# Moving the weight pages of a one-core encoder block to 96 bytes past a 128-byte boundary

## The chip, the core and the metric

The kernel runs on one core of a Trainium2 chip. The metric is the device time of one execution in microseconds, the median of several runs. One further execution is profiled: its page and its trace give, for every instruction of every engine, when it started and how long it took. TensorE does the matmuls (PE in the profile; its weight loads are listed apart as PEld), VectorE is DVE, ScalarE is ACT, GpSimd is POOL and SyncE, which issues most transfers, is SP.

## The reference, cut to what matters

One layer of an encoder over 512 tokens of width 2048, all in float32:

```
h = rms_norm(x)
q_a, k_a, v_a, q_g, k_g, v_g, r_g, gate_lr = split(h @ w_in)
y_a = banded softmax attention(q_a, k_a, v_a)         # 16 heads of 64
y_g = rms_norm(gated linear attention(q_g, k_g, v_g, gate)) * silu(r_g)   # 4 heads
x = x + concat(y_a, y_g) @ w_out
u = causal_conv(rms_norm(x) @ w_ffn_up);  u_gate, u_val = split(u)
x = x + (gelu(u_gate) * u_val) @ w_ffn_down           # inner width 5632
x = x + sigmoid(rms_norm(x) @ w_ple_gate) * (p @ w_ple_proj)
return rms_norm(x)
```

Nearly all of the work is the products of a weight matrix with the 512 tokens. The change alters no arithmetic.

## The kernel before, in words

**Precision.** Each float32 operand of a large product is split in two parts that TensorE reads as its fast float32 type (`F32R`): a rounded high part and the low rest. A product is then three matmuls: high by high, high by low, low by high. ACT writes the high part of a weight page (`wh`), DVE the low part (`wl`) as the difference (`prep_high`, line 447, and `prep_low`, line 470).

**Pages.** A page is a tile of 128 partitions by 1024 float32, 4096 bytes in each partition. The pool `pages` (line 49) holds 17 of them, one behind the other: `r0` to `r7` for raw weights, `u0`, `u1`, `c0` for results, and `h0` to `h2` and `l0` to `l2` for the high and low parts of the weights that TensorE reads. Seven more pages (`c1`, `x0`, `x1`, `u2`, `u3`, `c2`, `r8`, the tuple `LATE`) lie in the pool `late` at the right end of the memory and are opened after the attention.

**The first 330 us.** `vproj` (line 228) computes values with the weights streaming: in lines 250 to 252 the moving operand is a page `wh` or `wl`, 512 columns wide, and the stationary one is 128 columns of an input tile `h1` (pool `h`, 16 tiles of 4096 bytes, `slot`, line 203). There are 4 calls (two column halves for each of two value matrices), each with 16 blocks of the inner dimension, 4 blocks of tokens and 3 matmuls. `proj` (line 137, through `mm3`, line 132) is turned round: the page is stationary, an input tile is the moving operand, 512 columns wide; 8 calls of 16 blocks and 3 matmuls. One more product, `plr` (lines 1077 to 1080), reads its stationary columns from a page at steps of 128 bytes.

**The rest.** All later weight products run by a seven-product Strassen scheme in stages: `in`, `wo`, `up`, three `dn`, `pg` (class `Stage`, line 312). A unit is two blocks of 128 output rows. Its operands from the token side (`R11`, `R21`, `N2`, `N1`, `T3`, `R22`, `T4`) were combined beforehand, stored to device memory, and are loaded per stage into tiles of 128 x 2 x 1024 float32, 8192 bytes in each partition: six in the pool `xa` at the right, eight in the pool `xb` at the left (`xtile`, line 299), `xb` taking over the room of `h`. `product` (line 482) issues the matmuls: for an ordinary product three passes over `kb` inner blocks (8, or 7 in two of the `dn` stages), moving 256 columns of an operand tile over 128 columns of `wh` or `wl` (line 513); in the units between the first two and the last two of a stage, three of the seven products are joined (line 502): high by (high and low) in one matmul of 512 columns from two places of the operand tile, then low by high in 256 columns (line 504).

In the last stage three tiles of the pool `xa` that are no longer needed serve as pages for the weights of the last products (`EARLY`, line 936, and lines 1270 to 1273; their name is `last`).

**Order.** Each engine takes its instructions in the order in which the kernel issues them; from line 1248 on the order on DVE, ACT and TensorE is that of the loop over `steps` (line 1250), where the weights of step i + 2 are prepared before the product of step i.

**Where the tiles lie.** The left side grows upward from constants and scratch; the right side grows downward from the end. Two tiles exist only to set addresses: `shim` (240 float32, 960 bytes, line 1036) at the right end before everything else there, and `pad` (8 float32, 32 bytes, line 1223) at the start of `xb`. The byte offsets in each partition come to:

| tiles | first byte | past a multiple of 128 | past a multiple of 512 |
|---|---|---|---|
| `pages` | 15360 | 0 | 0 |
| input tiles `h1` | 84992 | 0 | 0 |
| operand tiles in `xb` | 85024 | 32 | 32 |
| operand tiles in `xa`, so `last` too | 179232 | 32 | 32 |
| `late` pages | 150560 | 32 | 32 |
| attention tiles `Q`, `Kh`, `Kl` | 152352 and on | 32 | 288 |

Within a product all offsets go in steps of 512 bytes (stationary) and 1024 or 4096 bytes (moving), so a whole product has one pair of places.

Of the kernel before, what the change touches and what calls it, by code (L numbers as in the profile page):

```python
# [8 lines left out]
F32 = mybir.dt.float32  # L9
# [5 lines left out]
P = 128  # L15
# [27 lines left out]
def encoder_block(ctx: ExitStack, tc: tile.TileContext, A, out):  # L43
    nc = tc.nc
# [4 lines left out]
    pg = ctx.enter_context(tc.tile_pool(name="pages", bufs=1))  # L49
# [153 lines left out]
    def slot(i, name, dt=F32R):  # L203
        return hp.tile([P, 2, T], dt, tag=f"h{i}", name=name)

    pairs = [pg.tile([P, 2, T], F32, tag=t, name=f"pair_{t}") for t in PAIR_TAGS]

    def xslot(i, name):
# [54 lines left out]
    xa, xb = [], []  # L263
# [126 lines left out]
    def issue():  # L390
        kept, i = 0, 0
        while i < len(wanted):
            unit, name = wanted[i]
            if len(free) <= kept:
                return
            if name[-1] == "*":
                kept += 1
                i += 1
                continue
            wanted.pop(i)  # L400
            n = unit.stage.kb * P
            t = raw_page(unit, name)[:, :n]
            src = lambda q: unit.stage.weights(unit.u, q)
            if name[0] == "L":
                nc.sync.dma_start(t, src(name))
            else:
                nc.sync.dma_start(t, src("L21"))
                nc.gpsimd.dma_start(t, src("L22" if name == "S1" else "L11"), accum_op=ALU.add)  # L408
# [35 lines left out]
    def prep(i, own=None):  # L444
        prep_low(prep_high(i, own))
# [587 lines left out]
            (nc.scalar if c else nc.sync).dma_start(vad[4 * c:4 * c + 4, :, t].rearrange("b p v -> p b v"),  # L1033
                              vstage[c, t].rearrange("p (b v) -> p b v", b=4))

    shim = ctx.enter_context(tc.tile_pool(name="shim", bufs=1, side="right")).tile([P, 240], F32, tag="shim", name="shim")
    nc.gpsimd.memset(shim, 0.0)
    with ExitStack() as mix:
        vp = mix.enter_context(tc.tile_pool(name="v", bufs=1, side="right"))
# [180 lines left out]
    def operands_left():  # L1220
        hctx.close()
        xb.append(ctx.enter_context(tc.tile_pool(name="xb", bufs=1, reuse_waits="tile")))
        pad = xb[0].tile([P, 8], F32, tag="pad", name="pad")
        nc.gpsimd.memset(pad, 0.0)
        for op in ("N1", "T3", "R22", "T4"):
            for g in range(2):
                front.load(op, g)
        free.extend(("r0", "r1", "r2"))
        issue()
        prep(0)  # L1230
        prep(1)
        for g in range(2):
            front.split("N1", g)

    values_a(1, operand_step, operands_left)
    pctx.close()
    pp_ = ctx.enter_context(tc.tile_pool(name="banks", bufs=1, space=PSUM, reuse_waits="tile"))
# [194 lines left out]
```

## Time and profile before

| | us |
|---|---|
| three runs | 2314.81, 2318.54, 2322.06 |
| median of the runs | 2318.54 |
| span of the profiled execution, first to last instruction | 2315.0 |

The profiled execution's own time is its span and a little around it; the span lies within the spread of the three runs, 3.5 us under their median. The page gives, for each engine, its busy time and share of the span; then the span in slices; the transfers; the chain of work that ended last; and the costliest groups of instructions with count, total busy time and mean duration. Matmuls overlap one another on TensorE, so the duration of one (279 ns in many groups) is not what it costs: that is the distance from its start to the start of the next, which the timeline of the engine gives. There a row is a run of equal instructions: start of the first, time from there to the end of the last, what it is, and how many.

### The profile page before, as it was taken

What the parts mean: (1) busy time and instruction counts of PE and PEld (TensorE: products, weight loads), DVE (VectorE), ACT (ScalarE), POOL (GpSimd) and SP (SyncE); (2) the same over time, 40 slices, a digit from 0 to 9 for tenths busy, and PEclk for the clock granted to TensorE, in tenths of its full rate; (3) what the DMA queues carried; (4) which work ended last, traced back from release to release, by engine and by line L of the source; (5) the groups of instructions that cost most, each with busy time, mean ns of one, the idle gap of its engine ahead of it and who ended that gap; (6) DMA issues with size and microseconds to landing.
All of it is one profiled execution on the core that took longest, in us unless ns stands there. A gap on an engine that the chain in (4) does not pass through costs nothing.

```text
span 2315.0 us, 42243 instructions
## 1 busy us (share of the span) xinstructions
PE 2269.1 (98%) x16564; PEld 2122.6 (92%) x16564; DVE 1957.4 (85%) x2753; ACT 1295.4 (56%) x1894; POOL 143.1 (6%) x180
## 2 busy tenths in 40 slices
PE   9999999999999999999999999999999999999996
PEld 8878889999989999999999999999999999999995
DVE  7556358888779888999999999999898797999997
ACT  6344356777555565555555555555564554656655
POOL 0000000000000000000000000000000100000100
PEclk9999999999999999999999999999999999999998
DMA  6522486666978977787877777777866967879994
GB/s 221 195 76 88 168 286 168 177 182 185 314 244 269 309 219 201 214 220 213 219 211 214 206 218 207 218 210 217 261 213 222 316 216 250 282 241 331 273 288 160
DMA packets 195464, 516.48 MB, mean 223 GB/s; under 512 B 20896, under 2 KB 72352, under 8 KB 195264
## 3 DMA queue, kind: packets, MB, share of 16 engines
q1 hardware_dynamic: 165184, 421.49, 51.9%
q0 software_dynamic: 23616, 84.95, 20.8%
q10 hardware_dynamic: 6464, 7.34, 0.9%
q8 instruction: 130, 2.13, 0.4%
q14 instruction: 70, 0.57, 0.1%
HBM read 435.05 MB, written 76.55 MB: 221 GB/s over the span
## 4 chain that ended last, share of the span: by engine, by line
PE 86%; DVE 6%; DMA 4%; ACT 2%; issue 2%; ACTq 0%; DVEq 0%; SPq 0%; POOL 0%; POOLq 0%
PE accA L65 39%; PE accC L65 20%; PE accB L65 10%; PE v L250 2%; PE v L251 2%; PE v L252 2%; DVE wl L65 1%; DMA s<-in_w_blk 1%; DVE u L65 1%; PE pp L65 1%; PE py L65 1%; PE ptr L65 1%; DVE s L65 1%; PE psc L65 1%; PE pk L134 1%
## 5 line engine op out<-in xcount | busy, mean ns | idle before, releaser
L65 DVE TENSOR_TENSOR wl<-s,wh 128x1024 fp32r<-128x1024 f32 (+1 forms) x365 | 437.3, 1199 | 47.3 <-ACT wh L65 46.3
L65 ACT ACTIVATE wh<-l 128x1024 fp32r<-128x1024 f32 (+1 forms) x308 | 318.8, 1037 | 174.9 <-PE accC L65 110.2
L65 ACT ACTIVATE wh<-s 128x1024 fp32r<-128x1024 f32 (+1 forms) x365 | 377.6, 1037 | 48.1 <-DVE s L65 31.8
L65 DVE TENSOR_TENSOR wl<-l,wh 128x1024 fp32r<-128x1024 f32 (+1 forms) x308 | 367.8, 1194 | 39.8 <-ACT wh L65 39.5
L65 ACT ACTIVATE u<-accA 128x256 f32<-128x256 f32 x290 | 109.4, 377 | 339.1 <-PE accA L65 338.9
L65 DVE TENSOR_TENSOR s<-s,l 128x1024 f32<-128x1024 f32 (+1 forms) x192 | 229.5, 1195 | 13.9 <-DMA s<-in_w_blk 12.7
L65 PE MATMUL accA<-up_T,wh 128*128 128x256 f32 (+1 forms) x1088 | 178.6, 313 | 0.2 <-ACT u L65 0.2
L65 PEld LDWEIGHTS accA<-up_T,wh 128*128 128x128 f32 x1088 | 150.1, 188 | 11.4 <-ACT u L65 0.4
L65 DVE SCALAR_TENSOR_TENSOR cv<-u,cw,cv 128x511 f32<-128x511 f32 (+1 forms) x176 | 131.5, 747 | 3.1
L408 POOL DMA_DIRECT2D s<-in_w_up x88 | 75.1, 853 | 788.4 <-DVE u L65 256.7
L65 DVE TENSOR_TENSOR u<-u,accC 128x256 f32<-128x256 f32 x158 | 66.1, 418 | 44.2 <-PE accC L65 41.5
L251 PE MATMUL v<-wv_l,h 128*128 128x512 f32 x256 | 100.5, 392 | 0.0
L250 PE MATMUL v<-wv_h,h 128*128 128x512 f32 x256 | 100.3, 392 | 0.0
L252 PE MATMUL v<-wv_h,h 128*128 128x512 f32 x256 | 99.9, 391 | 0.0
L65 PE MATMUL accA<-up_T,wl 128*128 128x256 f32 x704 | 96.3, 279 | 0.0
L65 ACT ACTIVATE cv<-u,cw 128x512 f32<-128x512 f32 x88 | 67.1, 810 | 51.9 <-DVE u L65 51.9
L65 PEld LDWEIGHTS accA<-up_T,wl 128*128 128x128 f32 x704 | 91.2, 188 | 3.7
L65 PE MATMUL accA<-dn_T,wh 128*128 128x256 f32 (+1 forms) x616 | 90.4, 296 | 2.8 <-ACT wh L65 2.8
L65 PE MATMUL accB<-up_R,wh 128*128 128x512 f32 (+1 forms) x384 | 91.2, 380 | 1.9 <-DVE up_R L65 1.3
L65 PE MATMUL accA<-up_R,wh 128*128 128x256 f32 x704 | 89.7, 279 | 0.0
L65 PE MATMUL accA<-up_N,wh 128*128 128x256 f32 x704 | 89.3, 279 | 0.1
L65 PE MATMUL accC<-up_N,wh 128*128 128x256 f32 x704 | 89.2, 279 | 0.0
(386 smaller groups left out, 5123.2 us busy)
## 6 DMA issues: line engine op xcount, KB each, us to landing
l<-in_w_up SPq DMA_DIRECT2D x132, 512.0 KB, 5.1
s<-in_w_up SPq DMA_DIRECT2D x88, 512.0 KB, 4.6
s<-in_w_up POOLq DMA_DIRECT2D x88, 512.0 KB, 5.7
l<-in_w_dn SPq DMA_DIRECT2D x56, 448.0 KB, 5.0
l<-in_w_blk SPq DMA_DIRECT2D x36, 512.0 KB, 5.1
l<-in_w_out SPq DMA_DIRECT2D x28, 512.0 KB, 5.2
l<-in_w_dn SPq DMA_DIRECT2D x28, 512.0 KB, 5.3
s<-in_w_blk SPq DMA_DIRECT2D x24, 512.0 KB, 4.5
```

Source lines behind the costliest of these rows:

```text
L65: ins = f(*args, **kw)
L134: nc.tensor.matmul(po, whi, act[:, 1, :], start=False, stop=False)
L250: nc.tensor.matmul(ps[t], h1[kt][:, 0, sl], wh, start=kt == 0, stop=False)
L251: nc.tensor.matmul(ps[t], h1[kt][:, 0, sl], wl, start=False, stop=False)
L252: nc.tensor.matmul(ps[t], h1[kt][:, 1, sl], wh, start=False, stop=kt == KD - 1)
L408: nc.gpsimd.dma_start(t, src("L22" if name == "S1" else "L11"), accum_op=ALU.add)
```

## The change

A tile `lead` of 24 float32, 96 bytes in each partition, is put at the start of the pool `pages` and set to zero once. `pad` grows from 32 to 64 bytes and `shim` shrinks from 960 to 832 bytes.

```
+    lead = pg.tile([P, 24], F32, tag="lead", name="lead")
+    nc.gpsimd.memset(lead, 0.0)
     pairs = [pg.tile([P, 2, T], F32, tag=t, name=f"pair_{t}") for t in PAIR_TAGS]
...
-    shim = ctx.enter_context(tc.tile_pool(name="shim", bufs=1, side="right")).tile([P, 240], F32, tag="shim", name="shim")
+    shim = ctx.enter_context(tc.tile_pool(name="shim", bufs=1, side="right")).tile([P, 208], F32, tag="shim", name="shim")
     nc.gpsimd.memset(shim, 0.0)
...
-        pad = xb[0].tile([P, 8], F32, tag="pad", name="pad")
+        pad = xb[0].tile([P, 16], F32, tag="pad", name="pad")
         nc.gpsimd.memset(pad, 0.0)
```

The places that follow: everything in `pages` and `h` moves up by 96 bytes, the operand tiles in `xb` by 96 + 32 = 128, and everything on the right side by 128.

| tiles | first byte after | past a multiple of 128 | past a multiple of 512 |
|---|---|---|---|
| `pages` | 15456 | 96 | 96 |
| input tiles `h1` | 85088 | 96 | 96 |
| operand tiles in `xb` | 85152 | 32 | 160 |
| operand tiles in `xa`, so `last` too | 179360 | 32 | 160 |
| `late` pages | 150688 | 32 | 160 |
| attention tiles | 152480 and on | 32 | 416 |

No matmul, no copy, no transfer and no wait is added or taken away but the one memset of `lead`.

## The prediction

> **What bounds the kernel now.** I read the page first, then who TensorE waited for, then busy time by stage.
>
> ```profile
> span 2315.0 us, 42243 instructions
> PE 2269.1 (98%) x16564; PEld 2122.6 (92%) x16564; DVE 1957.4 (85%) x2753; ACT 1295.4 (56%) x1894; POOL 143.1 (6%) x180
> PE 86%; DVE 6%; DMA 4%; ACT 2%; issue 2%; ACTq 0%; DVEq 0%; SPq 0%; POOL 0%; POOLq 0%
> ```
>
> ```profile
> PE ms L65 <- ACT q L65: 4.8, 2, 2.7
> PE accA L65 <- DVE wl L65: 4.6, 5, 1.3
> ...
> PE pw L83 <- POOL ones L76: 1.2, 1, 1.2
> ```
>
> ```profile
> core 0: us, PE busy (x) PEld busy (x) DVE busy (x) ACT busy (x) POOL busy (x), PEclk, DMA share, GB/s
> 640.00:830.00 190.00, 183.94 (x1402) 176.02 (x1402) 164.60 (x220) 114.05 (x172) 11.96 (x14) 0.99 0.87 273
> 830.00:1700.00 870.00, 869.64 (x6487) 824.68 (x6486) 803.17 (x1024) 472.38 (x640) 75.08 (x88) 1.00 0.79 218
> 2000.00:2220.00 220.00, 213.99 (x1662) 205.93 (x1661) 206.11 (x283) 137.52 (x208) 13.66 (x16) 0.99 0.87 275
> ```
>
> TensorE is busy 98% of the span, its largest total wait is 4.8 us, and in the `up` stage (830 to 1700 us) it stands still for 0.4 us of 870. What moves the end is the pace at which TensorE starts matmuls, times their number. DVE, at 803 of 870 us, has 8% to spare there, and 6% in the `dn` stretch from 2000 us.
>
> The pace is read from starts on TensorE's timeline. First `up`, in the middle of the stage:
>
> ```profile
> 1202.58 2.03 PE L65 MATMUL accA<-up_T,wh 128*128 128x256 f32 x16
> 1204.45 1.09 PE L65 MATMUL accA<-up_T,wl 128*128 128x256 f32 x8
> 1205.38 2.03 PE L65 MATMUL accC<-up_R,wh 128*128 128x512 f32 x8
> 1207.25 1.09 PE L65 MATMUL accC<-up_R,wl 128*128 128x256 f32 x8
> ```
>
> 24 matmuls of 256 columns take 1205.38 - 1202.58 = 2.80 us, 116.7 ns each; 8 joined ones of 512 columns take 1.87 us, 234 ns each. At the start of the kernel, where page and input tile both begin at a multiple of 512, 512 columns cost less:
>
> ```profile
> 199.44 0.39 PE L135 MATMUL pk<-h,wkg_l 128*128 128x512 f32 x1
> 199.66 0.39 PE L133 MATMUL pk<-h,wkg_h 128*128 128x512 f32 x1
> ...
> 202.16 0.39 PE L135 MATMUL pq<-h,wqg_l 128*128 128x512 f32 x1
> ```
>
> From 199.44 to 202.16 there are 12 starts: 2.72 us / 12 = 226.7 ns. So the same number of columns costs 227 or 234 ns by where the operands lie. This is the lever that the change pulls.
>
> **The change part by part.** I write d for the moving operand's place less the stationary one's, modulo 512. For Strassen matmuls from pages d goes from 32 - 0 = 32 to 160 - 96 = 64. For `vproj`, `proj` and `plr` both operands move by 96 and d stays. For the `last` tiles both move by 128 and d stays 0.
>
> *Strassen matmuls of 256 columns.* An ordinary unit has 7 products x 3 passes x kb of them, a joined one 4 x 3 x kb + 3 x kb. With kb = 8: `in` 12 ordinary units, 2016; `wo`, `dn0`, `pg` four ordinary and four joined each, 1152; `up` four and forty, 5472; `dn1`, `dn2` with kb = 7, 1008 each. Sum 12,960, less 72 that read `last`: 12,888. So 1 ns on each is 12.9 us.
>
> The profile has no row at d = 64 with a stationary operand at 96, so I bound it. What the stationary place does is seen where the operand tiles serve as pages, d = 0:
>
> ```profile
> 2275.24 2.03 PE L65 MATMUL accC<-pg_N,wh 128*128 128x256 f32 x16
> 2277.11 1.09 PE L65 MATMUL accC<-pg_N,wl 128*128 128x256 f32 x8
> 2278.03 3.03 PE L65 MATMUL accC<-pg_N,last 128*128 128x256 f32 x24
> ```
>
> ```profile
> 486.53 0.28 PE L65 MATMUL psc<-Kh,Q 128*128 128x256 f32 x1
> ...
> 487.13 0.28 PE L65 MATMUL psc<-Kl,Q 128*128 128x256 f32 x1
> ```
>
> The `wh` row costs 1.87 us / 16 = 116.9 ns. In the `last` row the 24th matmul starts at 2278.03 + 3.03 - 0.28 = 2280.78, so 2.75 us / 23 = 119.6 ns. The attention's `psc` (Q and K both at 288 past 512, d = 0) makes 5 steps in 0.60 us, 120 ns. Same columns, 3.3 ns more: the upper end. The lower end is 113.3 ns, half of the 226.7 that 512 columns cost above. Between them lies a second pace at today's places:
>
> ```profile
> 775.00 2.05 PE L65 MATMUL accA<-wo_R,wh 128*128 128x256 f32 x16
> ...
> 780.65 2.05 PE L65 MATMUL accB<-wo_R,wh 128*128 128x256 f32 x16
> ```
>
> Two passes of 24 take 5.65 us, 117.7 ns, 1.0 more than in `up`. And `plr` steps the stationary place through 0, 128, 256 and 384 with two matmuls at each:
>
> ```profile
> 95.05 0.39 PE L1079 MATMUL plr<-h,glh 128*128 128x512 f32 x1
> ...
> 95.51 0.40 PE L1079 MATMUL plr<-h,glh 128*128 128x512 f32 x1
> 95.75 0.40 PE L1080 MATMUL plr<-h,glh 128*128 128x512 f32 x1
> 95.99 0.40 PE L1079 MATMUL plr<-h,glh 128*128 128x512 f32 x1
> 96.22 0.39 PE L1080 MATMUL plr<-h,glh 128*128 128x512 f32 x1
> ...
> 96.91 0.39 PE L1079 MATMUL plr<-h,glh 128*128 128x512 f32 x1
> ...
> 102.49 0.39 PE L133 MATMUL pk<-h,wkg_h 128*128 128x512 f32 x1
> ```
>
> All 32 take 7.44 us, 232.5 ns each against 226.7. From 95.51 to 96.22, at the places 128 and 256, it is 237 ns; from 96.22 to 96.91, where the weights being loaded reach 384 (d = 128), 230 ns. So larger d is no better than d = 0 and at 128 costs some 3 ns per 512 columns. The new d = 64 lies between 32 and 128. I take the second pace, 1.1 ns over the first, as the rows on both sides allow it: 12,888 x 1.1 = +14.2 us. The ends are -3.3 x 12,888 = -43 and +43 us.
>
> *Joined matmuls of 512 columns.* 24 per joined unit at kb = 8: `wo`, `dn0`, `pg` 96 each, `up` 960, `dn1` and `dn2` 84 each, 1416. They share the pages and d. With the same 1.1 ns: +1.6 us; ends by 226.7 and by 240 ns (twice 120): -10 and +9 us.
>
> *`vproj`, `proj`, `plr`.* 4 x 16 x 4 x 3 + 8 x 16 x 3 + 32 = 1184 matmuls of 512 columns. d is unchanged; I take 0. Should a moving operand off its multiple of 128 be what costs, each would go from 226.7 to the joined rows' 234 ns: +8.6 us. The lower end is 0, as 226.7 is the lowest that any row of 512 columns shows.
>
> TensorE's rule in the Trainium skill, "TensorE: Matmul & The Clock Gate", section "Part 2: What happens when you issue a matmul", speaks against all of this: the array has two independent read ports, and loading the next weights takes no read bandwidth from the running matmul. By it the sum would be 0; the 116.9 and 119.6 ns above, with one and the same moving tile, do not fit it.
>
> *DVE, ACT, transfers.* A copy or difference between the two kinds of places shows whether 32 bytes matter there: `last` is written at 32, `wh` and `wl` at 0, mostly from pages at 0.
>
> ```profile
> L65 ACT ACTIVATE last<-s x3: 1044/1045/1051, 2260.8 to 2274.3; 128x1024 fp32r<-128x1024 f32 x3
> L65 DVE TENSOR_TENSOR last<-s,last x3: 1216/1225/1227, 2263.5 to 2275.4; 128x1024 fp32r<-128x1024 f32 x3
> ```
>
> ```profile
> L65 ACT ACTIVATE wh<-s 128x1024 fp32r<-128x1024 f32 x309 | 324.6, 1053 | 30.1 <-DVE s L65 23.0 <-PE accB L65 6.1 <-PE accA L65 0.5
> ```
>
> ```profile
> L65 DVE TENSOR_TENSOR wl<-s,wh 128x1024 fp32r<-128x1024 f32 x309 | 376.5, 1219 | 34.5 <-ACT wh L65 33.6
> ```
>
> 1045 against 1053 and 1225 against 1219 ns: under 1%, both signs. I take 0; without DVE's 8% of slack the 6 ns over some 620 such differences would be 4 us. Weight pages now land at other bytes; TensorE's list of waits holds no transfer, so I take 0.
>
> "DMA: Bandwidth & Descriptors", section "How a descriptor splits into AXI transactions", of the Trainium skill says that a start off a multiple of 256 bytes costs one more transaction and the bytes before it. An estimate from it is 131 beats in place of 128 for a 4096-byte row, 2.3% on each weight load; no run here shows it, and it would stay behind TensorE's work.
>
> *`lead`.* One small memset on POOL. TensorE's one wait for POOL is for `ones` (L76), which stands ahead of it; POOL is busy 6%. 0 us; on the path it would be a fraction of that wait of 1.2 us.
>
> **Sum.** +14.2 + 1.6 + 0 = +15.8 us on the profiled execution's 2315.0. The runs' median lies 3.5 us above that span, so 2318.5 + 15.8 = 2334 us.
>
> **The rivals.** *Full collision (R1).* Any stationary operand off its multiple of 128 costs what `last` and `psc` show, 120 ns. For it: the only two rows with such a stationary operand both say 120. Against it: both have d = 0 too, so they don't separate place from distance. Sum: +43 + 9, and up to +8.6 from the start: 2318.5 + 52 = 2370.
>
> *Distance heals (R2), the other side.* Weight load and moving stream start together and get in one another's way when they lie close; d = 0 gives 120, d = 32 gives 116.7, and d = 64 goes on to 113.3 ns. For it: the two points lie on that line. Against it: `plr`, where d = 128 is dearer than d = 0. Sum: -43 - 10 = -53; it decides from the first Strassen matmul after 330 us. DVE would then be short: 206 us of work in the 220 of 2000 to 2220, which at 113.3 / 116.7 become 214. I give a fifth back: 2318.5 - 42 = 2276. A weaker form, 116.0 ns, gives about 2309.
>
> *Nothing (R3).* The new places run at the old pace in the old mixture: 2318.5. For it: the 116.7 ns of `up` holds over 870 us whatever DVE, ACT and the transfers do meanwhile. Against it: every other pair of places in the trace has a pace of its own. (The Trainium skill's rule on the two read ports, above, gives this time.)
>
> **How the numbers follow.** The likeliest is the forecast, 0.30, from 2326 to 2346. R1 has 0.27, R2 in full 0.21 and weak 0.13, R3 0.09. A measurement of this kernel can tell about 0.3%, 7 us, from no change. Slower: 0.30 + 0.27 = 0.57. Same: 0.09. Faster: 0.21 + 0.13 = 0.34. The range reaches up to R1 with half of its start, 2376, and down to R2, 2274, since both signs hold much of the chance; a fifth (most of R2's lower half, R1 with dearer joined matmuls) is left out.
>
> **What would show it.** In the timeline of `up`, the starts of 24 matmuls of 256 columns: 2.83 us is the forecast, 2.88 R1, 2.72 R2, 2.80 R3. The `last` row must stay at 2.75 us for 23 steps, as its d is unchanged; if it falls, the place and not the distance counts. `pk` must stay at 2.72 us for 12; 2.81 would put the cost on the moving operand's place. Copies of 1053 ns and differences of 1219 ns must not change. If TensorE's list of waits shows a transfer or DVE with tens of us, the sum was made on the wrong engine.

## The result and the profile after

| | before | changed |
|---|---|---|
| median of four runs, us | 2318.03 | 2306.80 |
| lowest to highest, us | 2314.81 to 2322.06 | 2305.10 to 2309.76 |
| span of the profiled execution, us | 2315.0 | 2305.5 |

The median of the kernel before now takes in a fourth run, 2317.52 us. The ratio is 0.9948, with an interval of 0.9934 to 0.9962: the changed kernel is faster by about half a per cent. The time lies inside the predicted range, on the other side of the forecast of 2334 us, 2 us from the rival's weak form (2309).

The head of the page of the changed kernel; its third line is the chain of work that ended last:

```profile
span 2305.5 us, 42244 instructions
PE 2255.2 (98%) x16564; PEld 2114.8 (92%) x16564; DVE 1957.7 (85%) x2753; ACT 1295.7 (56%) x1894; POOL 143.1 (6%) x181
PE 84%; DVE 7%; DMA 4%; ACT 2%; issue 2%; ACTq 0%; DVEq 0%; POOL 0%; SPq 0%; POOLq 0%
```

TensorE is still what sets the time: the same 16,564 matmuls and 98% of the span. DVE and ACT do the same work in the same time; the one new POOL instruction is the memset. The span fell by 9.5 us and TensorE's busy time by 13.9.

Where it went is seen in the timeline of TensorE in `up` (start, time from there to the end of the last of the row, what, count):

```profile
926.17 1.98 PE L65 MATMUL accA<-up_T,wh 128*128 128x256 f32 x16
...
928.89 1.99 PE L65 MATMUL accC<-up_R,wh 128*128 128x512 f32 x8
930.72 1.11 PE L65 MATMUL accC<-up_R,wl 128*128 128x256 f32 x8
931.66 2.00 PE L65 MATMUL accA<-up_T,wh 128*128 128x512 f32 x8
933.50 1.07 PE L65 MATMUL accA<-up_T,wl 128*128 128x256 f32 x8
...
937.12 1.99 PE L65 MATMUL accB<-up_R,wh 128*128 128x512 f32 x8
938.95 1.11 PE L65 MATMUL accB<-up_R,wl 128*128 128x256 f32 x8
939.90 2.04 PE L65 MATMUL accA<-up_N,wh 128*128 128x256 f32 x16
...
942.72 2.05 PE L65 MATMUL accC<-up_N,wh 128*128 128x256 f32 x16
```

The first 24 matmuls of 256 columns shown start within 928.89 - 926.17 = 2.72 us, 113.3 ns each, the pace of the rival "distance heals". After the next joined block the pace is another: 930.72 to 931.66 is 0.94 us for 8, 117.5 ns. After the second joined block it is 113.1 ns again (933.50 to 937.12, 32 matmuls in 3.62 us), and after the third 117.5 (939.90 to 942.72, 24 in 2.82 us). So there is not one pace at the new distance but two, 113.3 and 117.8 ns, and a block of eight joined matmuls changes from one to the other. Of the 120 such blocks in `up` 115 changed the pace; the other five left the slow one as it was. A unit has three blocks, an odd number, so the three ordinary products between its first block (`accB`) and its second (`accC`) fall on the fast pace in one unit and on the slow one in the next. The joined matmuls themselves went from 234 to 1.83 / 8 = 229 ns.

Summed over the whole trace, from each matmul's start to the next one's (steps of more than 0.3 us, 0.5 us for the longer matmuls, are counted as waits):

```
                                           before    changed    difference
us, 256 columns, `up`                       639.8      635.1          -4.7
us, 256 columns, all stages                1523.6     1515.1          -8.5
us, 512 columns joined, `up`                224.0      219.8          -4.2
us, 512 columns joined, all stages          330.4      324.5          -5.9
us, waits                                    53.2       58.5          +5.3
256-column matmuls in runs at 116.6 ns       9185          0
256-column matmuls in runs at 113.4 ns          0       4685
256-column matmuls in runs at 117.8 ns       2408       6942
```

(A run is twelve or more matmuls at one pace.) The last rows explain the size: (4685 x 113.4 + 6942 x 117.8) / 11,627 = 116.0 ns on average against 116.8 before. The three differences, -8.5, -5.9 and +5.3 us, come to -9.1 us; the span fell by 9.5. Some 5 us of the gain came back as waits, by TensorE's list of waits:

```profile
PE ms L65 <- ACT q L65: 5.7, 2, 3.4
PE accA L65 <- ACT wh L65: 5.4, 4, 2.7
...
PE accA L65 <- ACT u L65: 3.2, 4, 1.4
```

Waits for ACT's copies and evictions were 2.8 (`wh`), 1.7 (`u`) and 4.8 us (`q`) before: TensorE now arrives earlier at the edges of the stages and stands there.

The signs that the prediction named, in the same timeline at `last` and at `pk`, where d is unchanged though all places moved:

```profile
2268.34 3.03 PE L65 MATMUL accC<-pg_N,last 128*128 128x256 f32 x24
...
198.17 0.39 PE L133 MATMUL pk<-h,wkg_h 128*128 128x512 f32 x1
...
200.89 0.39 PE L133 MATMUL pq<-h,wqg_h 128*128 128x512 f32 x1
```

`last` has (3.03 - 0.28) / 23 = 119.6 ns as before, and `pk` makes 12 steps in 2.72 us as before. And the groups of copies and differences, by form (busy us, mean ns):

```profile
L65 ACT ACTIVATE wh<-s 128x1024 fp32r<-128x1024 f32 x309 | 324.2, 1052 | 32.7 <-DVE s L65 25.2 <-PE accB L65 5.3 <-issue 1.0
...
L65 DVE TENSOR_TENSOR wl<-s,wh 128x1024 fp32r<-128x1024 f32 x309 | 376.8, 1221 | 32.2 <-ACT wh L65 31.4
```

1052 against 1053 and 1221 against 1219 ns: neither engine notices the 96 bytes.

### The profile page after: what moved, and what is told of

The parts are those of the page before. It is cut to its first block, busy times and chain, and to the rows that moved or that the text cites. A ratio compares the mean times of both kernels' runs of the same rounds, so it can differ in the third digit from the quotient of the medians.

```text
span 2305.5 us, 42244 instructions
## 1 busy us (share of the span) xinstructions
PE 2255.2 (98%) x16564; PEld 2114.8 (92%) x16564; DVE 1957.7 (85%) x2753; ACT 1295.7 (56%) x1894; POOL 143.1 (6%) x181
## 3 DMA queue, kind: packets, MB, share of 16 engines
q1 hardware_dynamic: 165184, 421.49, 52.5%
## 4 chain that ended last, share of the span: by engine, by line
PE 84%; DVE 7%; DMA 4%; ACT 2%; issue 2%; ACTq 0%; DVEq 0%; POOL 0%; SPq 0%; POOLq 0%
PE accA L65 38%; PE accC L65 20%; PE accB L65 10%; PE v L252 2%; PE v L253 2%; PE v L254 2%; DVE wl L65 2%; DVE s L65 1%; DVE u L65 1%; PE py L65 1%; PE psc L65 1%; PE ptr L65 1%; PE pk L134 1%; DMA wo_T<-mix_T 1%; PE pk L133 1%
```

## The experiments

Throughout, "narrow" is a matmul of 256 columns, "joined" one of 512 columns from two places of the moving tile, and d the moving place less the stationary one. The three kernels of matmuls alone (`pace_map`, `pace_states`, `short_loads`) ran once each.

**Matmuls alone, every distance.** `pace_map` leaves the encoder block out: after one load it runs only matmuls, for four stationary places (0, 32, 64, 96) and sixteen distances each, 40 narrow, 8 joined, 32 narrow, 8 joined, 32 narrow, 7 joined, 32 narrow, 1 joined, 24 narrow. The tile `s96d64p` is stationary place 96, d = 64.

```
for i, (s, d) in enumerate((s, d) for s in (0, 32, 64, 96) for d in range(0, 512, 32)):
    m = (s + d) % 512
    ps = pp.tile([P, T], F32, tag=f"b{i % 7}", name=f"s{s}d{d}p")
    narrow(ps, s, m, 40)
    joined(ps, s, m, 8)
    narrow(ps, s, m, 32)
    ...
```

> A kernel of matmuls alone: it computes nothing of the block. One stationary page and one moving tile; for each of 64 pairs (stationary place s = 0, 32, 64, 96 past a multiple of 512; distance d = moving place less s, 0 to 480 in steps of 32) it issues 40 matmuls of 256 columns, then 8 joined of 512, 32 narrow, 8 joined, 32 narrow, 7 joined, 32 narrow, 1 joined, 24 narrow. Theory 1 (distance, two locked paces): at d = 64 the narrow runs go at 113.3 or 117.8 ns whatever s is, and change between the two behind blocks of 8 joined; at d = 32 116.7 (or 117.8), at d = 0 120; the four s agree. Theory 2 (place): the paces differ by s; d = 64 with s = 0 does not show 113.3. Theory 3 (other engines, transfers): with nothing beside TensorE all narrow runs go at one pace, 113.3 or less, at every d.

The timeline of TensorE, the first rows of tiles at the stationary places 0 and 96:

```profile
18.97 4.96 PE L38 MATMUL s0d0p<-X,W 128*128 128x256 f32 x40
...
43.67 4.83 PE L38 MATMUL s0d32p<-X,W 128*128 128x256 f32 x40
...
67.93 4.70 PE L38 MATMUL s0d64p<-X,W 128*128 128x256 f32 x40
72.47 1.99 PE L47 MATMUL s0d64p<-X,W 128*128 128x512 f32 x8
74.30 3.93 PE L38 MATMUL s0d64p<-X,W 128*128 128x256 f32 x32
...
79.90 3.79 PE L38 MATMUL s0d64p<-X,W 128*128 128x256 f32 x32
...
91.96 4.96 PE L38 MATMUL s0d96p<-X,W 128*128 128x256 f32 x40
...
165.70 4.71 PE L38 MATMUL s0d192p<-X,W 128*128 128x256 f32 x40
...
1238.65 4.70 PE L38 MATMUL s96d64p<-X,W 128*128 128x256 f32 x40
```

In each row, the time less the last matmul's own 0.28 us, over 39 steps, is the pace: for d = 64 (4.70 - 0.28) / 39 = 113.3 ns.

```
d                       0      32      64      96     128     160     192     224
narrow, ns          120.0   116.7   113.3   120.0   118.7   117.4   113.6   118.2
also seen there                     117.8                           117.8
```

The table gives all eight distances at the stationary place 0; rows for the places 32, 64 and 96 agree (`s96d64p` beside `s0d64p`), and from 256 on the sequence repeats. So the pace hangs on the distance alone, with a period of 256 bytes, and it is not monotone: 113.3 at 64 stands between 116.7 and 120.0. The alternation of the changed kernel is here as well, with DVE idle, ACT busy for 0.6 of 1583 us and the transfers at 1% of their engines: narrow rows of 32 at d = 64 take 3.93 us after the first joined block (117.8 ns) and 3.79 after the second (113.2). Joined matmuls cost 232 to 233 ns at d = 32 and 228 to 229 at d = 64, the difference that the changed kernel shows. The theories of the place, and of other engines, fall.

**The same distance from the old pages.** `pages0_operands64` leaves the pages at 0 and moves only the operand tiles, from 32 to 64.

```
-    shim = ... .tile([P, 240], F32, tag="shim", name="shim")
+    shim = ... .tile([P, 232], F32, tag="shim", name="shim")
...
-        pad = xb[0].tile([P, 8], F32, tag="pad", name="pad")
+        pad = xb[0].tile([P, 16], F32, tag="pad", name="pad")
```

> Pages and input tiles stay at 0 as before, the Strassen operands go from 32 to 64, so d = 64 as in the changed kernel but with the stationary operand on a multiple of 512. Theory 1 (distance): like the changed kernel, ratio to before 0.993 to 0.997, about 2307 us, runs of 113.3 and of 117.8 ns in turn. Theory 2 (place): no gain, 2318 us or more.

2306.62 us (2305.87 to 2310.94), ratio 0.9961 [0.9947, 0.9975]. Narrow matmuls of `up` sum to 634.8 us, joined ones to 219.8 (changed kernel: 635.1 and 219.8). Its timeline in `up`:

```profile
1208.28 2.04 PE L65 MATMUL accA<-up_R,wh 128*128 128x256 f32 x16
...
1211.10 2.00 PE L65 MATMUL accB<-up_R,wh 128*128 128x512 f32 x8
1212.94 1.07 PE L65 MATMUL accB<-up_R,wl 128*128 128x256 f32 x8
1213.85 1.98 PE L65 MATMUL accA<-up_N,wh 128*128 128x256 f32 x16
```

24 matmuls in 2.82 us (117.5 ns), a joined block, then 8 in 0.91 us (113.8). The two ratios' intervals overlap: d = 64 gives the gain from the old pages too, and no effect of the 96 bytes by themselves is seen.

**No joined matmuls.** `changed_all_narrow` and `before_all_narrow` are the two kernels with the joined products issued as three narrow passes.

```
-JOINED = ("P2", "P3", "P4")
+JOINED = ()
```

> The changed kernel with no joined matmuls: every product in three passes of 256 columns. Theory 1: without joined blocks nothing moves TensorE from one locked pace to the other in the middle of a stage, so the up stage stays at the pace in which it begins: at 113.3 ns the whole ends near 2290 us, at 117.8 near 2325 us; hardly any change of pace within a stage. Theory 3 (the slow runs come from other engines or transfers): the mixture stays as in the changed kernel, about 2307 us, with changes of pace in the middle of stages.

> The kernel before with no joined matmuls, d = 32. Theories 1 and 3: two matmuls of 256 columns at 116.7 cost what one joined one of 512 costs at 233.3, so 2316 to 2322 us, the same as before within 0.3%; it shows that leaving out the joining is worth nothing by itself.

The changed one took 2323.54 us (2321.25 to 2328.81), ratio 1.0037 [1.0021, 1.0052]: slower than the kernel before. Its timeline in `up`:

```profile
1204.30 2.05 PE L65 MATMUL accC<-up_N,wh 128*128 128x256 f32 x16
...
1207.13 2.04 PE L65 MATMUL accA<-up_T,wh 128*128 128x256 f32 x16
```

24 starts in 2.83 us. In runs, 14,828 narrow matmuls go at 117.8 ns and 193 at 113.4: without joined blocks the pace did not change again in `up`, and this kernel sat on the slow one. The kernel before, all narrow, took 2322.69 us (2316.14 to 2324.89), ratio 1.0021 [1.0009, 1.0032]: within 0.3%, though on the slower side. There 7430 narrow matmuls went at 116.67 and 7439 at 117.8, so d = 32 has two paces too, only 1.1 ns apart.

**Which block changes the pace.** `pace_states` is again matmuls alone: at d = 64 and 192, blocks of 1 to 9 joined matmuls between rows of 32 narrow ones (the tile `d64j6p` has blocks of six), and then 512 columns in one piece at every distance.

```
for d in (64, 192):
    for c in range(1, 10):
        narrow(ps, 0, d, 32)
        for _ in range(4):
            joined(ps, 0, d, c)
            narrow(ps, 0, d, 32)
```

> A second kernel of matmuls alone, computing nothing of the block; stationary operand at 0. For d = 64 and 192 and for c = 1 to 9: 32 narrow matmuls of 256 columns, then four times c joined of 512 and 32 narrow. Then, for d = 0 to 224 in steps of 32, 24 matmuls of 512 columns in one piece. Theory 1 (two locked paces that a block of joined matmuls changes by its length): at d = 64 the joined matmuls go round in threes, so blocks of 3, 6 and 9 leave the pace as it was and blocks of 8 change it; at d = 192 blocks of 8 keep 113.3. Rival (the change comes with any stall or switch of form, not with the count): all c behave alike at one d. For 512 columns in one piece theory 1 expects the lowest, 226.7 ns, at d = 0, where the kernel's first 330 us run, and 230 ns or more elsewhere.

Its timeline, the rows around the first block of six at d = 64, and of eight at d = 192:

```profile
127.22 3.93 PE L37 MATMUL d64j6p<-X,W 128*128 128x256 f32 x32
130.99 1.55 PE L46 MATMUL d64j6p<-X,W 128*128 128x512 f32 x6
132.37 3.79 PE L37 MATMUL d64j6p<-X,W 128*128 128x256 f32 x32
...
383.24 3.79 PE L37 MATMUL d192j8p<-X,W 128*128 128x256 f32 x32
386.86 2.02 PE L46 MATMUL d192j8p<-X,W 128*128 128x512 f32 x8
388.73 3.79 PE L37 MATMUL d192j8p<-X,W 128*128 128x256 f32 x32
```

A row of 3.93 us is the slow pace, (3.93 - 0.28) / 31 = 117.7 ns, one of 3.79 the fast one, 113.2. At d = 64, blocks of 3, 6 and 9 kept a fast pace, and one of 6 and one of 9 turned the slow pace into the fast one; 1, 4 and 7 ended on the slow one, and 2, 5 and 8 ended now here, now there (of the four blocks of eight, two left the slow pace as it was). At d = 192, blocks of an even number ended on the fast pace and those of an odd number changed it. In one piece, 512 columns cost 226.6 ns at d = 0, once the row has settled, and 228.7 to 234.3 elsewhere, so d = 0 is among the dearest for 256 columns and the cheapest for 512.

**The distance 192.** At d = 192 the kernel's blocks of eight should leave the fast pace alone. `pages0_operands192` is the kernel before with `shim` at 200 and `pad` at 48 floats; `pages0_operands192_narrow` has `JOINED = ()` besides.

```
-    shim = ... .tile([P, 240], F32, tag="shim", name="shim")
+    shim = ... .tile([P, 200], F32, tag="shim", name="shim")
...
-        pad = xb[0].tile([P, 8], F32, tag="pad", name="pad")
+        pad = xb[0].tile([P, 48], F32, tag="pad", name="pad")
```

> Pages and input tiles at 0, Strassen operands at 192: d = 192. In the matmul kernel this distance gave 113.3 ns also behind blocks of 8 joined, and 232.7 ns for a joined one. Theory 1: the up stage holds 113.3 ns once it has it and loses only about 4 ns on each joined matmul, so 2292 to 2302 us, ratio 0.989 to 0.994, below the changed kernel. If it gets caught at 117.8 and stays, 2318 or more. Rival (the gain needs the new places of the changed kernel, or the rest of the program gives it back): 2307 or more.

> The same with all products in passes of 256 columns. Theory 1: no blocks to leave 113.3, so 2285 to 2295 us if the stages begin at 113.3, about 2323 if they begin at 117.8 as in the changed kernel without joined matmuls.

The first took 2292.79 us (2291.70 to 2293.21), ratio 0.9898 [0.9883, 0.9913], about twice the gain of the change. Its timeline in `up`:

```profile
1210.72 1.98 PE L65 MATMUL accA<-up_T,wh 128*128 128x256 f32 x16
...
1213.44 2.02 PE L65 MATMUL accC<-up_R,wh 128*128 128x512 f32 x8
1215.30 1.07 PE L65 MATMUL accC<-up_R,wl 128*128 128x256 f32 x8
1216.21 2.02 PE L65 MATMUL accA<-up_T,wh 128*128 128x512 f32 x8
```

113.3 ns ahead of the joined block (24 in 2.72 us) and after it (8 in 0.91). In runs, 9093 narrow matmuls are at 113.4 and 2832 at 117.8; most of the slow ones lie in the stage `in`, which has no joined block, and in `dn1` and `dn2`, whose blocks are of seven. In `up` the slow pace comes in five times, three times behind a wait or a late start of TensorE and twice behind a joined block, and each time one of the next two joined blocks ends it. One such stretch, behind a wait of 0.54 us for ACT:

```profile
973.91 2.15 PE L65 MATMUL accA<-up_N,wh 128*128 128x256 f32 x16 [0.54 <-ACT u L65]
...
976.84 2.05 PE L65 MATMUL accC<-up_N,wh 128*128 128x256 f32 x16
...
979.67 2.05 PE L65 MATMUL accA<-up_T,wh 128*128 128x256 f32 x16
```

24 matmuls from 976.84 take 2.83 us (117.9 ns); the joined block at 982.50 ends it. So the blocks of eight do more here than leave the fast pace alone: they bring it back.

The narrow form took 2311.85 us in the middle of ten runs, ratio 0.9957 [0.9925, 0.9990], but these reach from 2284.81 to 2317.76. In the profiled one `up` ran at 118.0 ns and `dn1` at 113.45. The start of `up` in its timeline:

```profile
807.06 1.98 PE L65 MATMUL accA<-up_R,wh 128*128 128x256 f32 x16
...
811.77 1.47 PE L65 MATMUL accB<-up_R,wh 128*128 128x256 f32 x8 [1.38 <-ACT up_R L65]
...
820.35 2.05 PE L65 MATMUL accA<-up_N,wh 128*128 128x256 f32 x16
...
823.17 2.05 PE L65 MATMUL accA<-up_N,wh 128*128 128x256 f32 x16
```

The stage begins on the fast pace ((1.98 - 0.28) / 15 = 113.3 ns); behind the waits for the operand tiles it is slow (24 in 2.82 us), and with no block to bring the fast pace back it stays so to the end of the stage. Only one of the ten runs was traced, so it is likely, but not shown, that their spread comes from the pace on which each stage settled.

**Blocks of another length.** To keep one pace in the real kernel, only the first `NJ` inner blocks of a joined product are joined, the others run in three narrow passes. `changed_joined6` is the changed kernel with 6; `d192_joined2` is `pages0_operands192` with 2 (even, so that all of the `dn` stages keep the pace); `d192_joined2_front` joins two in the stage `in` as well.

```
-            for p in range(2):
+            for p in range(3):
...
-                    w = (hi, lo)[p][:, k * P:k * P + P]
-                    if p == 0:
+                    w = (hi, hi, lo)[p][:, k * P:k * P + P]
+                    if p == 0 and k < NJ:
...
-                    else:
-                        ten.matmul(t, w, x[:, 0], start=False, stop=k == kb - 1, skip_group_check=True)
+                    elif p != 1 or k >= NJ:
+                        ten.matmul(t, w, x[:, p % 2], start=False, stop=p == 2 and k == kb - 1, skip_group_check=True)
```

and for the stage `in`:

```
+                for u in self.units if weights is front_weights else ():
+                    u.joined = JOINED
```

> The changed kernel (d = 64) with one number altered: of the 8 (or 7) inner blocks of a joined product only the first 6 are joined, the others go in three passes of 256 columns. The same arithmetic. In the matmul kernel blocks of 6 at d = 64 bring 117.8 back to 113.3 and keep 113.3, blocks of 8 change it each time. Theory 1: nearly no run at 117.8 in up, 2280 to 2292 us, ratio 0.984 to 0.989. Rival (the full kernel's changes of pace come from something else than the length of the joined block): the mixture stays, about 2307.

> Pages at 0, operands at 192 (d = 192), joined blocks of 2 instead of 8 or 7. In the matmul kernel blocks of an even number at d = 192 leave 113.3 in any case. A joined matmul costs 6 ns over two narrow ones, so blocks of 2 save about 6 x 6 x 3 = 110 ns a unit against blocks of 8, and the dn stages with 7 inner blocks no longer change pace. Theory 1: 2276 to 2288 us, ratio 0.982 to 0.987. Rival (only the distance counts, the blocks don't): the same as with blocks of 8, 2293.

> The same, and the first Strassen stage (in, 330 to 640 us) joins 2 inner blocks in three of its seven products too, which it did not before. Theory 1: the stage's runs at 117.8 behind the attention's small matmuls end at the next such block; at most 2000 x 4.4 = 9 us less than without, likely 2 to 6 us, 2272 to 2284 us. Rival: DVE, which adds a second half for each joined product (0.42 us, 36 times), delays the stage: the same or more.

| kernel | us | ratio | narrow at 113.4 | at 117.8 |
|---|---|---|---|---|
| changed, 6 joined | 2320.64 (2316.06 to 2324.13) | 1.0005 [0.9994, 1.0015] | 1086 | 11,710 |
| d = 192, 2 joined | 2289.29 (2285.95 to 2291.74) | 0.9870 [0.9856, 0.9885] | 12,467 | 1835 |
| d = 192, 2 joined, `in` too | 2286.63 (2284.93 to 2287.72) | 0.9859 [0.9844, 0.9874] | 13,189 | 1179 |

The first missed its expectation. Its timeline in `up` (a row of ten "128x512" is six joined matmuls and the first four narrow ones behind them):

```profile
1202.17 2.05 PE L66 MATMUL accA<-up_T,wh 128*128 128x256 f32 x16
...
1205.00 2.00 PE L66 MATMUL accC<-up_R,wh 128*128 128x512 f32 x10
1206.85 1.10 PE L66 MATMUL accC<-up_R,wl 128*128 128x256 f32 x8
1207.79 2.01 PE L66 MATMUL accA<-up_T,wh 128*128 128x512 f32 x10
```

The pace ahead of the block is 117.9 ns (24 in 2.83 us) and after it 117.5: blocks of six do keep the pace, as expected, but they kept the slow one, on which the stage began. That they turn slow into fast, which the matmuls alone had shown once, happened once here too (at 991 us). The other three changes of pace in `up` stand at steps that are 0.05 to 0.34 us too long (887, 901 and 1000 us), one into the fast pace and two out of it. The run also shows from the other side what the change lives on: with the alternation gone, d = 64 gives no gain at all.

At d = 192 both kernels came out a little above their numbers. Two joined in place of eight moved nearly everything to the fast pace, and in `up` the sum of narrow and joined fell from 848.0 to 841.4 us, more than the 110 ns a unit that the expectation counted (4.4 us for 40 units). What is missing went to waits: in the profiled executions the steps of narrow and joined matmuls fell by 9 us over all stages and the waits rose by 10 us, mostly in `dn`, `pg` and `up`, so that both spans are 2290.0 us. Joining two in `in` took its sum from 239.5 to 236.3 us. The last kernel has the lowest median: 1.4% under the kernel before, and 0.9% under the changed one by the quotient of the two ratios. Its interval overlaps that of the one without the joining in `in`, so what this last step adds is not clear of the noise. Its list of waits now has 6.2 us each for `wh` and `wl`.

**Shorter weight loads.** `short_loads` is matmuls alone, 256 columns over a stationary operand of 128, 64 or 32 columns, 64 in a row at each distance: if loading the next weights collides with the moving stream, a quarter of the load should have a quarter of the cost.

```
for cols in (128, 64, 32):
    for d in range(0, 256, 32):
        ...
        w = W[:, k % 8 * P:k % 8 * P + cols]
        nc.tensor.matmul(ps[0:cols, 0:256], w, X[:, o:o + 256], start=True, stop=True)
```

> A third kernel of matmuls alone, computing nothing of the block: for stationary operands of 128, 64 and 32 columns and for d = 0 to 224 in steps of 32, 64 matmuls of 256 moving columns, every stationary operand at a multiple of 512. If what costs is the weight load of the next matmul getting in the way of the moving stream (it reads 512 bytes of each partition with 128 columns, 256 and 128 bytes with 64 and 32), the spread of the paces over d, 113.3 to 120 ns with 128 columns, shrinks with the columns, and the slowest pace falls. Rival (a price of each change of stationary operand, or of the moving operand's place alone): the paces over d stay as they are with 128 columns.

Three rows of its timeline, then all paces (from one row's start to the next one's, over 64):

```profile
19.16 7.84 PE L68 MATMUL cols128d0p<-X,W 128*128 128x256 f32 x64
...
79.53 7.44 PE L68 MATMUL cols64d0p<-X,W 128*64 128x256 f32 x64
86.80 7.78 PE L68 MATMUL cols64d32p<-X,W 128*64 128x256 f32 x64
```

```
d                 0      32      64      96     128     160     192     224
128 columns   120.0   117.8   117.8   119.8   118.8   117.3   113.4   118.3
 64 columns   113.6   119.1   116.7   118.3   116.7   116.7   113.3   116.7
 32 columns   117.8   117.0   116.7   117.5   115.5   117.7   113.8   117.5
```

Which distance is dear changes with the number of stationary columns (d = 0 falls from 120.0 to 113.6 ns with half of them). That the weight load is what does it is likely, but not shown: fewer stationary columns also mean fewer rows of results. The spread does not shrink in proportion (6.6, 5.8 and 4.0 ns), and d = 192 stays between 113.3 and 113.8 throughout. Each case is one row, and with 128 columns d = 32 and d = 64 are caught here on the slower of their two paces, so single values of the table say little. The simple form of a collision isn't confirmed, and a collision isn't excluded. What in TensorE makes the two paces stays open.

## Why the prediction was right in part and wrong in its sign

*What bounds the kernel, and the lever: right.* Nothing but the steps between matmuls' starts moved by more than the 5 us of waits, and `pace_map` and `pages0_operands64` show that the distance d decides, not the place. Taking 0 for `vproj`, `proj` and `plr` held (`v` sums to 174.1 us before and after, `pk` to 44.9), as did 0 for DVE and ACT. The transfers stayed off the path as well: the packets of the busiest queue took 0.7% more time (51.9% of 2315.0 us before, 52.5% of 2305.5 after), and TensorE's list of waits again holds none.

*The narrow term: wrong, and with it the sign.* The step "I take the second pace, 1.1 ns over the first, as the rows on both sides allow it" gave +14.2 us; measured are -8.5. It made three errors. It placed d = 64 between the rows of d = 32 and d = 128 as though the pace ran smoothly between them; the map shows 116.7, 113.3, 120.0, 118.7 in a row, so two points say nothing of a third. Its point at d = 128 was moreover a row of 512 columns (`plr`), and `pace_states` finds 512 columns in one piece dearer at d = 128 than at 0 (232.3 against 226.6 ns) where narrow ones are cheaper (118.7 against 120.0). And it read the `wo` row of 117.7 ns as a pace that another distance could have: it is the second of the two paces that d = 32 itself has. The forecast's 117.8 does exist at d = 64, and the changed kernel with all products narrow, held there, is slow (2323.54); in the changed kernel joined blocks throw 4 in 10 of the matmuls to 113.4. So what it lacked is that the pace at a distance can have two values, and that the joined blocks, which it counted only for their own columns, choose between them.

*The joined term: wrong in sign too, and smaller.* "With the same 1.1 ns: +1.6 us" against -5.9: the joined matmuls fell from 234 to 229 ns, near the lower bound of 226.7 that the prediction quoted from `pk`. Carrying the narrow matmuls' difference over to them had no row behind it; `pace_map` shows the same fall, from 232 to 233 ns at d = 32 to 228 to 229 at d = 64.

*The lead, the waits: nearly right.* The memset shows nowhere. The cover that the prediction gave to DVE and ACT was thinner at the edges of stages than it said for a faster TensorE: 5 us came back.

*The rivals.* R1, the full collision for any stationary operand off its multiple of 128, falls with `s96d64p` at 113.3 ns. R2, "distance heals", had the right lower end, 113.3 ns, and its weak form the right average, 116.0 against a measured 116.0 in the runs. That its reason, the line from 120 over 116.7 to 113.3, led there was luck: the next point on the map is 120 again, and the average comes from an alternation that it did not know. Nor does d = 64 in full bring its 2276 us; a kernel at d = 192 that keeps the fast pace comes to 2286.63. R3, nothing, falls: the interval ends at 0.9962. The sum of 0 by the rule on the two read ports ("TensorE: Matmul & The Clock Gate", section "Part 2: What happens when you issue a matmul", of the Trainium skill) fell with it; with nothing but matmuls running, the same instruction went at 113.3 to 120.0 ns by distance, and in `short_loads` the number of stationary columns mattered to it. Whether the two reads hinder one another, which that rule denies, no run here separates.

## What to carry to other kernels

Where a chain of equal matmuls sets the time, treat the pace at the actual pair of operand places as something to be measured: a short kernel of matmuls alone, over the distances between moving and stationary operand, gives it at once, and neighbours don't predict it. Then look at what interrupts the row, since a distance can have two paces and a wait or a block of other matmuls may switch them; here the better of two places with the same lowest pace was the one where the blocks brought the fast pace back. Where runs of one kernel spread widely, a pace that a stage falls into by chance is one thing to look for.

## What the runs showed of the hardware that was not expected

- The pace of 256-column matmuls repeats with 256 bytes of distance and goes from 113.3 (d = 64, 192) to 120.0 ns (d = 0, 96), 6%; for 512 columns in one piece the order is another, 226.6 ns at d = 0 and up to 234.3 at 160 (`pace_map`, `pace_states`).
- At d = 64 and 192 a row of matmuls locks into 113.3 or 117.8 ns, at d = 32 into 116.7 or 117.8, and can hold it for a whole stage (nearly all of `up` at 117.8 ns in `changed_all_narrow`). Eight joined matmuls at d = 64 switched it 115 times in 120 in `up` of the changed kernel; in `pace_states` an even number at d = 192 brought or kept the fast one. A wait can switch it too, as the 0.54 us for ACT did in `pages0_operands192`.
- One and the same kernel (d = 192, all narrow) took from 2284.81 to 2317.76 us in ten runs, 1.4%, at granted clocks that all lay close together (0.991 to 0.995). One of them was traced, and it holds stages on either pace.
- Weight pages that begin 96 bytes past a multiple of 128 cost ACT, DVE and TensorE's own 512-column products nothing: 1052 against 1053 ns, 1221 against 1219, and 2.72 us for 12 steps of `pk` both times.
